# Two experts' tokens by halves of the sequence, in blocks that share one set of weights

## Chip, cores and metric

One core of one Trainium2 chip runs the whole program. The metric is the device time of one launch in microseconds; the kernel before took 1599.58 us (median of three runs, 1597.01 to 1599.73).

## What is computed

A decoder block on 1024 tokens of width 1024. A token mixer with two recurrent branches is followed by a mixture of experts and a final normalisation. Only the second part matters here:

```
g_logits = xf @ rg_w + rg_b;  grp = argmax(g_logits)            # 4 groups
e_logits = (xf @ re_w + re_b).reshape(T, 4, 8)
top_p, top_i = top_k(softmax(e_logits[t, grp]), 2)               # 2 experts of the group's 8
y[t] = sum over the 2:  weight * (silu(xb @ w_gate[e]) * (xb @ w_up[e])) @ w_down[e]
out = rmsnorm(h + y)
```

All is float32. There are 32 experts; the three matrices of one expert are 6 MB, and all of them, some 201 MB, are read from HBM in every launch.

## The kernel before

After the two branches, a loop `for hv in range(2)` (L971) takes the tokens in two halves of 512. For each half it does the up-projections (L997 to L999), then the output projection in four column quarters (`for q in range(4)`, L1012; matmuls L1025 to L1027). In the last quarter `begin` and `finish` (L934, L945) work off one chunk of 128 tokens at a time: transposes, norm, router logits `plg` (L950 and L957, float32 matmuls 128x36), and the normalised rows to `hf_dr` in HBM.

**Routing** runs in three groups of chunks, `GROUPS = ((0, 4), (4, 7), (7, 8))`. `choose` finds the two experts of each token, `place` counts ranks within an expert with two matmuls (L884, L885) and makes one-hot rows `oht` of each token's position; `spread` (L841) multiplies them with token numbers into a table `ptb`, one column of row numbers per expert. `pick` (L1070) then ranks the experts by their counts, writes the ranked expert numbers to `pei`, and `ranked` (L1092) permutes the table; `weigh` (L1108) does the same for the mixing weights.

**Blocks.** Three experts (29 to 31) are fixed: their weights are fetched before the counts are known, and each takes a block of up to 112 tokens. Of the other 29 the 11 with most tokens take full blocks (one of them a second one), and the other 18 share nine *paired* blocks, two experts with up to 64 tokens each. A full block splits each weight tile in a high and a low float32r part (`split`, L60 on ScalarE, L61 on VectorE) and does three matmuls of 512 columns; a paired block (`pair_mm`, L1356) multiplies the raw float32 tiles, with 64 stationary columns for each of the two experts. So a full block reads 6 weight tiles, a paired block 12.

**Weight tiles.** A tile is 128x2048 float32, 1,048,576 bytes (1.0486 MB); there are 192. `fetch` (L1240) puts them in order into a ring of 11 buffers (`rawxl`, `rawtg`, `rawoh`, `rawbo`, `rawxh`), whose memory earlier stages have used. All are issued in order from SyncE's queue: L1406 for experts known beforehand, L1413 for ranked ones, whose number SyncE first reads from `pei` into a register (L1410). A buffer comes free when its tile has been split, or when the pair's matmuls have read it.

**Order.** The program loops over 23 steps: three fixed blocks, then a pair followed by one or two full blocks, and a pair at the end. In step n it emits the gate and up matmuls (`pgu`), the next block's gather of rows from `hf_dr` by POOL (`gather`, L1263) and their transposes (`pxg`), and then the down matmuls (`pyd`) of step n-1 and the scatter-add of its result. A tile scheduler moves instructions within each engine's queue; each queue is then worked off in order. `overflow` (L1132, at n == 3) builds tables for blocks that did not fit; its loop at the end is entered only if there are any.

Of the kernel before, what the change touches and what calls it, by code (L numbers as in the profile page):

```python
# [9 lines left out]
F32 = mybir.dt.float32  # L10
# [22 lines left out]
def block_kernel(ctx, tc, x, meta_tokens, hg_lb_logits, norm_mix_g, w_in, gd_conv_w, gd_A_log, gd_dt_bias,  # L33
# [193 lines left out]
    ND = NE - 3  # L227
    NF = 11
# [590 lines left out]

    def first_max(name, vals, n, hot):  # L820
# [14 lines left out]
    def spread(oh, dst, n, ps=None, groups=GROUPS):  # L835

        ps = pr("ptb") if ps is None else ps
        for g in groups:
            for a in range(2):
                for c in range(*g):  # L840
                    nc.tensor.matmul(ps[:, 0:n], oh[a][:, c], dst[:, a * NC + c],  # L841
                                     start=(a == 0 and c == 0), stop=(a == 1 and c == NC - 1))
        return ps[:, 0:n]

    def choose(c0, c1):
# [5 lines left out]
        V.tensor_scalar(goh, goh, 1.0e30, -1.0e30, op0=ALU.mult, op1=ALU.add)  # L851
# [24 lines left out]
    def place(c0, c1):  # L876
# [22 lines left out]

    H = SEQ // 2  # L900
    ges = []
# [43 lines left out]
    def finish(cc, h2, hT, hf, ss):  # L945
# [3 lines left out]
        for k in range(6):  # L949
            nc.tensor.matmul(pl[:, 0:36], hT[:, k], wrt[:, k], start=(k == 0), stop=False)  # L950
# [5 lines left out]
        for k in range(6, 8):  # L956
            nc.tensor.matmul(pl[:, 0:36], hT[:, k], wrt[:, k], start=False, stop=(k == 7))  # L957
# [13 lines left out]
    for hv in range(2):  # L971
# [11 lines left out]
        for n in range(8):  # L983
# [7 lines left out]
            for j in range(2):  # L991
# [3 lines left out]
                for k in range(4):  # L995
# [9 lines left out]
                                   op0=ALU.mult, op1=ALU.subtract)  # L1005
        h2s = []
# [4 lines left out]
        for q in range(4):  # L1011
# [6 lines left out]
            qs = slice(q * 256, (q + 1) * 256)  # L1018
            for c in range(4):
# [16 lines left out]
        if hv == 0:  # L1036
            routed(*GROUPS[0])
    place(*GROUPS[1])
    ptb = pr("ptb")
    oht = ohts  # L1040
    spread(oht, ohb1, NE, ptb, GROUPS[:2])
    routed(*GROUPS[2])
    spread(oht, ohb1, NE, ptb, GROUPS[2:])


    tabi = r_("tabi", [P, NB], I32)
    wsl = r_("wsl", [P, NB])
    emp = r_("emp", [P, NB])

    def rows(ps, s):  # L1050
        V.tensor_scalar(emp[:, s], ps, 0.0, None, op0=ALU.is_equal)
        return V.scalar_tensor_tensor(tabi[:, s], emp[:, s], BIG, ps, op0=ALU.mult, op1=ALU.add)
# [3 lines left out]
    tabbed = rows(ptb[:, ND:NE], slice(NW, NBB))  # L1056
    tab1 = r_("tab1", [P, NE])
    V.tensor_copy(tab1, ptb[:, 0:NE])
    pei = r_("pei", [1, NE], I32)
    pef = r_("pef", [1, NE])  # L1060
    rowb = r_("rowb", [CL, NPR], I32)
# [8 lines left out]
    def pick(after):  # L1070

        with tc.issue_after(after.ins):
# [14 lines left out]
            t = ranked(tab1)  # L1087
            rows(t[:, 0:NW], slice(0, NW))
            V.tensor_scalar(ktmp[0:CL, 0:NPR], t[0:CL, NW:], 0.0, None, op0=ALU.is_equal)
            return V.scalar_tensor_tensor(rowb, ktmp[0:CL, 0:NPR], BIG, t[0:CL, NW:], op0=ALU.mult, op1=ALU.add)  # L1090

    def ranked(t):  # L1092
# [5 lines left out]
        o = ps[:, 256:256 + NW + NPR]  # L1098
# [4 lines left out]
        nc.tensor.matmul(o[0:CL, NW:], tT[:, 0:CL], perm[:, NF + NPR:ND], start=True, stop=True, skip_group_check=True)  # L1103
# [4 lines left out]
    def weigh(after):  # L1108

        with tc.issue_after(after.ins):  # L1110
# [12 lines left out]
            pw = spread(oht, ohw.rearrange("p a b e -> p a (b e)"), 2 * NE)  # L1123
            V.tensor_copy(tab1, pw[:, 0:NE])
            V.tensor_tensor(tab1, tab1, pw[:, NE:], op=ALU.add)
            V.tensor_copy(wsl[:, NW:NBB], tab1[:, ND:NE])
            V.tensor_copy(wsl[:, 0:NW], ranked(tab1)[:, 0:NW])
# [4 lines left out]
    def overflow():  # L1132

# [15 lines left out]
        V.tensor_tensor(pos, pos, psx, op=ALU.add)  # L1149
        gtx = r_("gtx", [P, NE, NT])  # L1150
# [72 lines left out]
    sx = mix.tile([P, 4, 1024], F32R, name="sx", tag="xh1")  # L1223
    whs = [sx[:, i] for i in range(2)] + [wp.tile([P, 1024], F32R, name=f"mwh{i}", tag="wh") for i in range(2)]
    wls = [sx[:, i + 2] for i in range(2)] + [wp.tile([P, 1024], F32R, name=f"mwl{i}", tag="wl") for i in range(2)]
    wls.append(tl.tile([P, 1024], F32R, name="mwl4", tag="gffn"))
# [11 lines left out]
    ring = list(range(len(raws)))  # L1238
# [10 lines left out]
    def raw(load, src, q):  # L1249
        nuse[0] += 1  # L1250
        return early.pop(0) if early else fetch(load, src, q)

    def wload(load, src, q):
        wr = raw(load, src, q)
        r = []
        for g in range(2):
            wh, wl = whs[next_("h", len(whs))], wls[next_("l", len(wls))]
            with tc.issue_after(tabbed.ins) if nuse[0] <= 6 else ExitStack():
                split(wh, wl, wr[g])
# [327 lines left out]
```

## Time and profile before

| what | value |
|---|---|
| runs | 1599.58, 1599.73, 1597.01 us |
| the profiled execution | 1599.57 us, span 1597.8 us |
| mean granted TensorE clock | 0.974 |
| busy: TensorE, VectorE, ScalarE, POOL | 94%, 50%, 34%, 12% |
| moved by DMA | 360.88 MB, of it 307.51 MB read from HBM |

The profile's times are counted from the span's start. Busy TensorE time is modelled: rows of matmuls overlap, so the distance between starts, not a row's duration, tells how fast they follow each other. A DMA share of 1.0 means that all 16 DMA engines worked all the time.

### The profile page before, as it was taken

The numbers are of one execution on the slowest core, as the hardware profiler recorded it, in microseconds if no ns is written. First come the engines' busy times: TensorE is split into PE (matmuls) and PEld (weight loads), VectorE is DVE, ScalarE is ACT, GpSimd is POOL, SyncE is SP. The second block draws the span as 40 slices with busy tenths as digits, with TensorE's granted clock in tenths as the row PEclk, the third lists the DMA queues.
The fourth block names the chain that finished last, engine by engine and source line by source line (L and its number), as shares of the span: only waits on it lengthen the run. The fifth ranks groups of instructions, "written<-read, shape, count | busy, mean of one in ns | idle before, by whom it ended". The sixth has DMA issues, their size and how long they took to land. (4 is left out here: it accounts for less than half of the span.)

```text
span 1597.8 us, 25202 instructions
## 1 busy us (share of the span) xinstructions
PE 1497.6 (94%) x9915; PEld 1136.9 (71%) x9915; DVE 803.1 (50%) x1512; ACT 540.8 (34%) x884; POOL 191.1 (12%) x161
## 2 busy tenths in 40 slices
PE   6999999999999999999999997898998988999984
PEld 6989898789888777778889797665545543655542
DVE  7223665458547638132455745865444431533635
ACT  6122321331232232223234323552444431533533
POOL 2050000010000001000000102115111111111013
PEclk9999999999999999999999997898999999999996
DMA  6264344335135324327765655798999999999995
GB/s 214 68 178 149 94 138 136 100 116 167 61 115 146 104 87 116 108 84 250 254 180 182 204 176 211 253 354 340 390 393 390 402 390 384 377 373 398 405 342 205
DMA packets 193387, 360.88 MB, mean 226 GB/s; under 512 B 29416, under 2 KB 136106, under 8 KB 168689
## 3 DMA queue, kind: packets, MB, share of 16 engines
q1 hardware_dynamic: 171872, 319.61, 56.1%
q0 software_dynamic: 6416, 16.42, 4.3%
q10 hardware_dynamic: 14976, 23.21, 4.2%
q8 instruction: 79, 1.29, 0.3%
q14 instruction: 44, 0.35, 0.1%
HBM read 307.51 MB, written 57.94 MB: 229 GB/s over the span
## 5 line engine op out<-in xcount | busy, mean ns | idle before, releaser
L287 PE MATMUL pj<-xh,wh 128*128 128x512 f32 (+2 forms) x832 | 307.5, 370 | 0.0
L289 PE MATMUL pj<-xh,wl 128*128 128x512 f32 (+2 forms) x832 | 306.9, 369 | 0.0
L288 PE MATMUL pj<-xl,wh 128*128 128x512 f32 (+2 forms) x832 | 305.7, 367 | 0.0
L287 PEld LDWEIGHTS pj<-xh,wh 128*128 128x128 f32 x832 | 156.7, 188 | 17.0 <-issue 0.2
L289 PEld LDWEIGHTS pj<-xh,wl 128*128 128x128 f32 x832 | 156.8, 188 | 16.6 <-issue 0.6
L288 PEld LDWEIGHTS pj<-xl,wh 128*128 128x128 f32 x832 | 156.6, 188 | 15.9
L347 ACT ACTIVATE st<-pj 128x512 f32<-128x512 f32 (+2 forms) x104 | 54.8, 527 | 169.7 <-PE pj L289 160.2
L61 DVE TENSOR_TENSOR wl<-wr,wh 128x1024 fp32r<-128x1024 f32 x44 | 53.7, 1221 | 85.4 <-ACT wh L60 75.4
L311 POOL TENSOR_TENSOR rn<-ss,mhalf 128x4 f32<-128x4 f32 x16 | 20.9, 1304 | 536.5 <-DVE ss L322 304.9
L60 ACT ACTIVATE wh<-wr 128x1024 fp32r<-128x1024 f32 x44 | 46.6, 1059 | 109.8 <-PE pj L288 97.6
L1025 PE MATMUL pyo<-wo,mm 128*128 128x256 f32 x256 | 73.5, 288 | 4.9 <-ACT mm L1003 4.9
L1026 PE MATMUL pyo<-wo,mm 128*128 128x256 f32 x256 | 72.8, 285 | 0.0
L1027 PE MATMUL pyo<-wo,mm 128*128 128x256 f32 x256 | 72.5, 285 | 0.0
L1358 PE MATMUL pgu<-rawxl,xTp 128*64 128x512 f32 x208 | 65.3, 604 | 4.8 <-DMA rawxl<-in_w_up_dram 4.8
L1371 DVE TENSOR_TENSOR msg<-msg,pgu 128x512 f32<-128x512 f32 x9 | 6.2, 688 | 119.8 <-PE pgu L1358 111.7
L1294 PE MATMUL pgu<-mwl,xTs 128*112 128x512 f32 x144 | 57.6, 401 | 2.3 <-DVE mwl L61 2.2
L1400 POOL DMA_INDIRECT h_dr<-h,tabi x23 | 37.8, 1643 | 167.8 <-ACT h L1336 86.6
L1025 PEld LDWEIGHTS pyo<-wo,mm 128*128 128x128 f32 x256 | 49.0, 192 | 5.3 <-ACT mm L1003 5.3
L997 PE MATMUL pup<-oh,uwh 128*128 128x512 f32 x128 | 51.8, 405 | 0.3 <-ACT uwh L60 0.3
L998 PE MATMUL pup<-ol,uwh 128*128 128x512 f32 x128 | 51.7, 404 | 0.0
L999 PE MATMUL pup<-oh,uwl 128*128 128x512 f32 x128 | 51.3, 402 | 0.3 <-DVE uwl L61 0.3
L1292 PE MATMUL pgu<-sx,xTs 128*112 128x512 f32 x120 | 49.6, 413 | 1.9 <-ACT sx L60 1.7
(651 smaller groups left out, 3272.9 us busy)
## 6 DMA issues: line engine op xcount, KB each, us to landing
rawxl<-in_w_up_dram SPq DMA_DIRECT2D x26, 1024.0 KB, 20.4
rawxl<-in_w_down_dram SPq DMA_DIRECT2D x23, 1024.0 KB, 21.1
wr<-in_w_in_dram SPq DMA_DIRECT2D x44, 512.0 KB, 4.5
rawxl<-in_w_gate_dram SPq DMA_DIRECT2D x22, 1024.0 KB, 24.8
rawxh<-in_w_down_dram SPq DMA_DIRECT2D x14, 1024.0 KB, 19.7
rawoh<-in_w_gate_dram SPq DMA_DIRECT2D x13, 1024.0 KB, 11.2
rawoh<-in_w_up_dram SPq DMA_DIRECT2D x12, 1024.0 KB
rawbo<-in_w_down_dram SPq DMA_DIRECT2D x12, 1024.0 KB, 22.3
```

The lines of the kernel that those rows point to most:

```text
L61: return eng.tensor_tensor(out=lo, in0=src, in1=hi.bitcast(F32), op=ALU.subtract)
L287: nc.tensor.matmul(ps[:, :n], wh[:, k], a, start=(k == 0), stop=False)
L288: nc.tensor.matmul(ps[:, :n], wh[:, k], b, start=False, stop=False)
L289: last = nc.tensor.matmul(ps[:, :n], wl[:, k], a, start=False, stop=(k == KD - 1))
L347: act(out=st[:, :n], in_=ps, func=func, scale=scale)
L997: nc.tensor.matmul(ps, wh[:, kk], oh[:, kk], start=(k == 0), stop=False)
L998: nc.tensor.matmul(ps, wh[:, kk], ol[:, kk], start=False, stop=False)
L1025: nc.tensor.matmul(ps[:, 0:256], mm[0][:, k, ts], wo[:, 0, k], start=(k == 0), stop=False)
L1026: nc.tensor.matmul(ps[:, 0:256], mm[0][:, k, ts], wo[:, 1, k], start=False, stop=False)
L1027: nc.tensor.matmul(ps[:, 0:256], mm[1][:, k, ts], wo[:, 0, k], start=False, stop=(k == 7))
L1294: nc.tensor.matmul(ps[:CB], xTh[:, kk], wl[:, s], start=False, stop=(kk == 7))
L1358: nc.tensor.matmul(ps[hs], lhsT[:, hs], w[2][:, s], start=start, stop=stop, skip_group_check=True)
```

## The change

The fixed experts are two now, 30 and 31 (`ND = 30`), and 12 experts instead of 11 take full blocks (`NF = 12`); nine pairs stay. Experts 30 and 31 together take two paired blocks: one for the tokens of the first half of the sequence, one for those of the second, each with up to 64 tokens of either expert, and the second uses the 12 weight tiles that were fetched for the first (`kept`). The table of the first half's block is spread at the end of hv == 0, its rows are gathered in hv == 1 into the buffer `rawtg` (tile `b1`), and are transposed ahead of the last quarter. The ring starts with 12 buffers (`rawxh` has four), and after 12 fetches goes on with `rawtg` and ten of them. The router's logits are computed in two halves of 64 tokens. The tables of `overflow` are split off and stand two steps later, behind that step's matmuls. The addition into `xg` (L1540) moves into the loop for overflow. Cut to its core:

```diff
-    ND = NE - 3
-    NF = 11
+    ND = NE - 2
+    NF = 12
...
-    def spread(oh, dst, n, ps=None, groups=GROUPS):
+    def spread(oh, dst, n, ps=None, groups=GROUPS, first=True, last=True):
...
+    def second(a, b):
+        return V.tensor_copy(tabB[CL:P, a - NF:b - NF], tabi[CL:P, a:b])
+    def fixed_rows(t, c):
+        for hs, e in zip(HALVES, (ND + 1, ND)):
+            V.tensor_copy(tabf[hs], t[hs, e:e + 1])
+        return rows(tabf, slice(c, c + 1))
...
         for k in range(6):
-            nc.tensor.matmul(pl[:, 0:36], hT[:, k], wrt[:, k], start=(k == 0), stop=False)
+            for hs in HALVES:
+                nc.tensor.matmul(pl[hs, 0:36], hT[:, k, hs], wrt[:, k], start=(k == 0), stop=False, skip_group_check=True)
...
+        if hv:
+            b1 = rawp.tile([P, 2, D], F32, name="b1", tag="tg")
+            nc.gpsimd.memset(b1[:, 0], 0.0)
+            gather(b1[:, 0], tabi[:, NW:NW + 1], P, H)
...
+            if hv and q == 3:
+                b1T = pair_x(b1[:, 0], b1[:, 1].rearrange("p (k t) -> p k t", k=KD))
...
         if hv == 0:
             routed(*GROUPS[0])
+            oht = ohts
+            V.tensor_copy(n0, off[:, 4, ND:])
+            V.tensor_copy(off[:, 4, ND:], off[:, 0, ND:])
+            ptb = spread(oht, ohb1, NE, groups=GROUPS[:1])
+            V.tensor_copy(tab1, ptb)
+            fixed_rows(tab1, NW)
+            second(NW, NW + 1)
     place(*GROUPS[1])
...
-    tabbed = rows(ptb[:, ND:NE], slice(NW, NBB))
+    tabbed = fixed_rows(ptb, NW + 1)
+    V.tensor_tensor(tab1, tab1, ptb[:, 0:NE], op=ALU.add)
...
-            pw = spread(oht, ohw.rearrange("p a b e -> p a (b e)"), 2 * NE)
+            for i, g in enumerate((GROUPS[:1], GROUPS[1:])):
+                pw = spread(oht, ohw.rearrange("p a b e -> p a (b e)"), 2 * NE, groups=g)
...
-    for pool, tag, n, b in ((mix, "xl", 4, 1), (rawp, "tg", 1, 1), (rawp, "oh", 2, 1), (tl, "bo", 2, 2), (mix, "xh0", 2, 1)):
+    for pool, tag, n, b in ((mix, "xl", 4, 1), (rawp, "oh", 2, 1), (tl, "bo", 2, 2), (mix, "xh0", 2, 1), (mix, "xh1", 2, 1),
+                            (rawp, "tg", 1, 1)):
...
+        if nraw[0] == NR:
+            ring[:] = [NR] + ring[:NR - 2]
...
-    steps = [(c,) for c in range(NBB - 1, NW - 1, -1)]
+    steps = [(NW,), (NW + 1,)]
...
         if c >= NW:
-            return by_expert(c - NW + ND)
+            loads = [by_expert(NE - 1), by_expert(ND)]
+            def both(src, q):
+                k = (src.tensor.name, q)
+                if k not in kept:
+                    kept[k] = [fetch(load, src, q) for load in loads]
+                return kept[k]
+            return both
...
-    xT = gathered(0)
-    first = xT[0][2]
+    xT = b1T
...
         if n == 0:
-            picked = pick(first)
+            picked = pick(tabbed)
+            weigh(picked)
...
         if n == 0:
-            weigh(picked)
+            down(*pend)
+            pend = None
         if n == 3:
             with tc.issue_after(picked.ins):
-                overflow()
+                over = overflow()
+        if n == 5:
+            with tc.issue_after(done_gu[0].ins):
+                overflow_tables(*over)
```

TensorE's queue at the end of the routing, before: the rank matmuls `prk`, the spreads into `ptb`, and then the first block (`pxg` are its transposes, `pgu` its gate matmuls).

```order
L884 MATMUL prk<-moh,ones 128x96
L885 MATMUL prk<-moh,tri 128x96
L841 MATMUL ptb<-ohb_7750,oht_8757 128x32 x4
L841 MATMUL ptb<-ohb_7750,oht_8758 128x32 x4
L841 MATMUL ptb<-ohb_7750,oht_8757 128x32 x3
L841 MATMUL ptb<-ohb_7750,oht_8758 128x32 x3
L884 MATMUL prk<-moh,ones 128x32
L885 MATMUL prk<-moh,tri 128x32
L841 MATMUL ptb<-ohb_7750,oht_8757 128x32
L841 MATMUL ptb<-ohb_7750,oht_8758 128x32
L1275 MATMUL pxg<-ident,h_9880 128x112 x8
```

The same place of the change (L886 and L887 are the rank matmuls, L843 the spread, L1408 the pair's matmuls, with `b_9197` the first half's transposed rows):

```order
L1408 MATMUL pgu<-rawxl,b_9197 64x512 x3
L1003 MATMUL plg<-wrt,hT 64x36 x4
L1408 MATMUL pgu<-rawxl,b_9197 64x512 x8
L886 MATMUL prk<-moh,ones 128x96
L887 MATMUL prk<-moh,tri 128x96
L1408 MATMUL pgu<-rawxl,b_9197 64x512 x5
L1408 MATMUL pgu<-rawoh,b_9197 64x512
L843 MATMUL ptb<-ohb_7752,oht_8799 128x32 x3
L843 MATMUL ptb<-ohb_7752,oht_8800 128x32 x2
L1408 MATMUL pgu<-rawoh,b_9197 64x512 x2
```

The gate and up matmuls of step 0 stand between the routing's matmuls. Behind these rows come one spread matmul, the second pair of `prk`, four `pgu`, the last two spread matmuls, and nine `pgu`; group 0's eight spread matmuls are gone from here.

TensorE's queue of the change somewhat later, from the last matmul of the weights' spread to the second block's up matmuls (`h_9978` are its gathered rows, `xTp_9991` their transposes; `phh` and `msg_9995` belong to step 0's hidden rows):

```order
L843 MATMUL ptb<-ohw,oht_8800 128x64
L1141 MATMUL prt<-ident,tab_7761 32x128
L936 MATMUL pxg<-ident,h_9978 128x128 x4
L1145 MATMUL prt<-perm,tT 128x12
L1147 MATMUL prt<-perm,tT 64x9 x2
L936 MATMUL pxg<-ident,h_9978 128x128 x4
L1429 MATMUL phh<-ident,msg_9994 128x128 x4
L1408 MATMUL pgu<-rawxl,xTp_9991 64x512
L1408 MATMUL pyd<-rawxh_9987,msg_9995 64x512 x8
L1408 MATMUL pyd<-rawxh_9988,msg_9995 64x512 x8
L1408 MATMUL pgu<-rawxl,xTp_9991 64x512 x15
```

The second block's transposes stand behind the permuted weights, and 16 down matmuls of step 0 stand in front of all but one of the second block's gate matmuls.

SyncE's queue of the change where the ranked experts begin:

```order
L1457 DMA rawxh_9988<-in_w_down_dram 128x2048 x2
L1461 TENSOR_LOAD pei
L1461 ISA x2
L1461 TENSOR_LOAD pei
L1461 ISA x2
L1464 ISA
L1464 DMA rawtg<-in_w_gate_dram 128x2048
L1461 TENSOR_LOAD pei
```

After two register loads and one fetch, the 28 other loads of expert numbers follow in one run, and the next fetch (into `rawxl`) stands behind them; before, the first ranked fetch stood behind six loads, and the others were scattered among later fetches.

## Rows read from the trace of the kernel before

**Rows 1.** The page's 40 slices, busy share of the DMA engines in tenths.

```profile
DMA  6264344335135324327765655798999999999995
```

**Rows 2.** Busy time by stretches: length, engines, granted clock, DMA share, GB/s.

```profile
980.00:1000.00 20.00, 8.56 (x48) 7.90 (x47) 15.23 (x70) 5.48 (x9) 8.75 (x7) 0.56 0.45 159
1000.00:1020.00 20.00, 16.07 (x67) 11.90 (x67) 14.19 (x23) 10.08 (x12) 2.98 (x3) 0.75 0.72 247
1020.00:1040.00 20.00, 19.81 (x112) 15.58 (x111) 18.37 (x45) 12.92 (x16) 2.02 (x2) 1.00 0.79 287
1060.00:1080.00 20.00, 20.00 (x98) 9.42 (x97) 9.10 (x10) 9.18 (x13) 2.55 (x2) 1.00 0.90 347
1100.00:1120.00 20.00, 19.69 (x80) 9.14 (x82) 4.40 (x11) 1.83 (x3) 7.34 (x9) 0.78 0.77 270
1120.00:1500.00 380.00, 356.06 (x1538) 196.65 (x1535) 163.96 (x168) 154.26 (x195) 54.32 (x38) 0.99 1.01 390
1350.00:1400.00 50.00, 47.31 (x213) 30.93 (x212) 26.62 (x27) 24.71 (x30) 4.24 (x3) 1.00 0.96 382
```

**Rows 3.** The same view, one stretch of 5 us.

```profile
1000.00:1005.00 5.00, 1.07 (x6) 1.10 (x7) 2.54 (x3) 0.05 (x1) 1.99 (x2) 0.50 0.75 249
```

**Rows 4.** Timeline of TensorE, routing: start, duration, instruction, [idle before, releaser].

```profile
981.99 1.71 PE L957 MATMUL plg<-wrt,hT 128*128 128x36 f32 x8
990.96 0.45 PE L884 MATMUL prk<-moh,ones 128*128 128x96 f32 x1 [7.26 <-DVE moh L860]
...
996.90 0.61 PE L841 MATMUL ptb<-ohb,oht 128*128 128x32 f32 x2 [1.22 <-DVE oht L898]
1003.93 1.73 PE L1275 MATMUL pxg<-ident,h 112*128 112x112 f32 x8 [6.42 <-DMA h<-hf_dr,tabi]
...
1018.94 0.21 PE L1081 MATMUL prk<-perm,pid 32*1 32x32 f32 x2
```

**Rows 5.** Timeline of TensorE, a pair's matmuls and the weights' spread.

```profile
1028.49 1.87 PE L841 MATMUL ptb<-ohw,oht 128*128 128x64 f32 x16
...
1064.12 3.60 PE L1358 MATMUL pgu<-rawbo,xTp 128*64 128x512 f32 x16
1067.56 3.60 PE L1358 MATMUL pgu<-rawxh,xTp 128*64 128x512 f32 x16
```

**Rows 6.** Timeline of VectorE, tables and picking.

```profile
997.74 0.16 DVE L1052 SCALAR_TENSOR_TENSOR tabi<-emp,ptb 128x3 int32<-128x3 f32 x1
...
1006.81 0.16 DVE L1073 TENSOR_SCALAR key<-keys 128x3 f32<-128x3 f32 x1
...
1008.04 0.23 DVE L1079 TENSOR_SCALAR perm<-io,rankc 32x32 f32<-32x32 f32 x1
...
1031.73 1.22 DVE L61 TENSOR_TENSOR sx<-rawbo,sx 128x1024 fp32r<-128x1024 f32 x1
...
1034.47 0.18 DVE L1127 COPY wsl<-prt 128x20 f32<-128x20 f32 x1
```

**Rows 7.** SyncE's register loads, line L1410, ns min/median/max, first and last start.

```profile
L1410 SPq TENSOR_LOAD <-pei x6: 267/272/477, 1020.6 to 1023.8; - x6
```

**Rows 8.** Timelines of POOL and TensorE, overflow tables.

```profile
1087.21 15.64 POOL L1185 TENSOR_SCALAR oht<-io,slot 128x128 fp32r<-128x128 f32 x16 [2.65 <-DVE xst L1166]
...
1096.76 0.61 PE L841 MATMUL ptb<-ohc,oht 128*128 128x72 f32 x4 [2.72 <-DVE ohc L1190]
```

**Rows 9.** Timeline of TensorE, logits 128 wide, and a short run 64 wide.

```profile
973.43 1.42 PE L950 MATMUL plg<-wrt,hT 128*128 128x36 f32 x12
974.68 1.07 PE L929 MATMUL phT<-ident,h 128*128 128x128 f32 x8
...
1034.04 0.28 PE L1101 MATMUL prt<-perm,tT 32*64 32x9 f32 x4
1034.18 0.26 PE L1103 MATMUL prt<-perm,tT 32*64 32x9 f32 x2
1034.36 0.49 PE L1293 MATMUL pgu<-mwh,xTs 128*112 128x512 f32 x1
```

More of the change, by code (lines that the diff above doesn't have):

```diff
@@ L833, in block_kernel @@
     ohef = ohe.rearrange("p a c e -> p (a c) e")
-    def spread(oh, dst, n, ps=None, groups=GROUPS):
+    def spread(oh, dst, n, ps=None, groups=GROUPS, first=True, last=True):
         ps = pr("ptb") if ps is None else ps
[L838 to L842, printed above, removed]
+        ac = [(a, c) for g in groups for a in range(2) for c in range(*g)]
+        for i, (a, c) in enumerate(ac):
+            nc.tensor.matmul(ps[:, 0:n], oh[a][:, c], dst[:, a * NC + c], start=first and i == 0,
+                             stop=last and i == len(ac) - 1)
         return ps[:, 0:n]
@@ L887, in place @@
             V.memset(off[:, 0], 0.0)
+            V.memset(off[:, 0, ND:ND + 1], float(CL))
         for c in range(HC):
@@ L956, in finish @@
         for k in range(6, 8):
-            nc.tensor.matmul(pl[:, 0:36], hT[:, k], wrt[:, k], start=False, stop=(k == 7))
+            for hs in HALVES:
+                nc.tensor.matmul(pl[hs, 0:36], hT[:, k, hs], wrt[:, k], start=False, stop=(k == 7), skip_group_check=True)
         V.scalar_tensor_tensor(lg[:, cc], pl[:, 0:36], rs, brt, op0=ALU.mult, op1=ALU.add)
@@ L1086, in pick @@
             V.tensor_scalar(nohx, ohx, -1.0, 1.0, op0=ALU.mult, op1=ALU.add)
[L1087 to L1090, printed above, removed]
+            rows(ranked(tab1), slice(0, NW))
+            return second(NF, NBB)
     def ranked(t):
@@ L1149, in overflow @@
         V.tensor_tensor(pos, pos, psx, op=ALU.add)
+        for a in range(2):
+            t8 = rp.tile([P, 4, 2], F32, name="t8", tag="t4")
+            V.tensor_tensor(t8, ohe[:, a, 4:, ND:], bc(n0[:, None, :], [P, 4, 2]), op=ALU.mult)
+            V.tensor_reduce(out=psx[:, a, 4:], in_=t8, op=ALU.add, axis=AX.X)
+        V.scalar_tensor_tensor(psx[:, :, 4:], pos[:, :, 4:], float(CB), psx[:, :, 4:], op0=ALU.is_ge, op1=ALU.mult)
+        V.tensor_tensor(pos[:, :, 4:], pos[:, :, 4:], psx[:, :, 4:], op=ALU.add)
         gtx = r_("gtx", [P, NE, NT])
@@ L1247, in fetch @@
         return wr
-    def raw(load, src, q):
-        nuse[0] += 1
-        return early.pop(0) if early else fetch(load, src, q)
     def wload(load, src, q):
-        wr = raw(load, src, q)
+        wr = fetch(load, src, q)
+        if not whs:
+            split_tiles()
         r = []
@@ L1338, in stage2 @@
         return pys
[L1341 to L1354 removed]
     def pair_mm(ps, lhsT, ws, s, start, stop):
         for hs, w in zip(HALVES, ws):
[L1358 removed]
+            mm = nc.tensor.matmul(ps[hs], lhsT[:, hs], w[2][:, s], start=start, stop=stop, skip_group_check=True)
+        return mm
     def pair_gu(xT, loads):
@@ L1384, in pair_down @@
         for q in range(2):
-            ws = [raw(load, wd_e, q) for load in loads]
+            ws = loads(wd_e, q)
             for k in range(2):
@@ L1450, in gathered, with places @@
         if paired(n):
-            return pair_x(*[got[i] for i in range(len(gq)) if gq[i][0] == n])
+            (xg,) = [got[i] for i in range(len(gq)) if gq[i][0] == n]
+            return pair_x(xg, xTp[next_("p", 2)])
         return [stage_x(got[i]) for i in range(len(gq)) if gq[i][0] == n]
-    for e, srcs in ((0, (wg_e, wu_e)), (1, (wg_e, wu_e)), (0, (wd_e,)), (2, (wg_e, wu_e))):
-        early += [(weights(e), src, q) for src in srcs for q in range(2)]
-    early = [fetch(*a) for a in early[:len(raws)]]
+    def places(c, n):
+        return [(tabi[:, c:c + 1], CL), (tabB[:, c - NF:c - NF + 1], P)] if paired(n) else [(tabi[:, c:c + 1], CB)]
     def down(n, *a):
@@ L1491, in block_kernel @@
     nc.sync.dma_start(out=gfin, in_=rowbc(final_norm_g[None, :], D))
-    idle = [i for i in range(len(raws)) if i not in ring] + ring
+    idle = [i for i in range(NR + 1) if i not in ring and i not in (NR - 2, NR - 1)] + ring
     accs = [raws[i] for i in idle[:NC]]
-    lridxs, lwcol = pend[1][0]
+    lplaces, lwcol = pend[1][0]
     LN = P if paired(len(steps) - 1) else CB
```

142 lines of the change are left out of this document (77 added, 65 removed).

## The prediction

> **What bounds the kernel now.** I read the page's 40 slices first, then the table of busy time by stretches, and only then timelines of the stretch in which the first expert blocks start. In the slices the reader sees the DMA share at nine tenths or more from about two thirds of the span on [rows 1]. The stretches say how full that is: from 1120 to 1500 us the engines are at 1.01 of their time and move 390 GB/s [rows 2]. So the expert blocks wait for weights: a tile of 1.0486 MB takes 1.0486 MB / 390 GB/s = 2.69 us there, while a full block's TensorE work is spread over six tiles and a pair's over twelve. TensorE's high busy share is no objection, since its rows overlap: eight pair matmuls follow each other in 3.44 us (1067.56 - 1064.12) though each row lasts longer [rows 5]. A pair's gate and up part is four such groups, 13.8 us of TensorE for eight tiles, which are 21.5 us of DMA.
>
> What can be saved therefore is time in which the DMA engines stand idle before the end. Before, that is 11.0 us of 980 to 1000, 5.6 of 1000 to 1020, 4.2 of 1020 to 1040, 2.0 of 1060 to 1080 and 4.6 of 1100 to 1120 [rows 2]. In the first of these the 11 buffers are full and no tile can be replaced; TensorE stands still for 7.26 us while VectorE chooses experts and for 6.42 us until the first gather lands [rows 4]. A tile's bytes are the same before and after, 192 tiles, so the change pays if the refill of the ring begins earlier, in proportion to what is loaded by then.
>
> **The change, part by part.** Times are in the clock of the trace before; the sum is against its profiled execution, 1599.57 us, which is also the median of the runs to 0.01.
>
> *Ahead of 984.* TensorE works without a gap here (no idle time stands in the first [rows 9]), so additions count in full. Eight spread matmuls of the first half move here from the routing: 16 of them took 1.87 us at most [rows 5], so 0.9 us. Eight transposes of the first half's block: 0.9 us (0.11 each, from the spacing of such rows in [rows 9], 974.68 on). The logits, in halves: 12 rows took 1.25 us 128 wide (974.68 - 973.43), 0.104 each; 64 wide, four rows take 0.14 us, 0.035 each, but the change of width costs about 0.11 (0.18 us until the next wide matmul, less two rows) [rows 9]. Per chunk there were 16 rows and are 32, with four changes of width: 32 x 0.035 + 4 x 0.11 - 16 x 0.104 = -0.1 us, for eight chunks -0.8. Bounds: without the cost of changes -4.4; if a 64-wide row took as long as a wide one, 8 x 16 x 0.104 = +13.3. I take the low price per row because that is the one row of this width with few columns. Sum of this part: **+1.0**. The memset and the gather of this block run on POOL at the start of the output projection and are covered by its first three quarters; the bytes are those of the first gather before.
>
> *Step 0 in the routing's gaps.* Eleven pair matmuls stand ahead of the first rank matmul: 11 x 0.43 = 4.7 us, inside the gap of 7.26. The six ahead of the spread wait beside VectorE's one-hot rows. Two and four more stand ahead of the last rank and spread matmuls and hold them by some 0.7 us: the last spread ends at 998.2, not 997.5 [rows 4]. Nine more take until 998.2 + 3.9 = 1002.1. The second block's rows can land as before, 6.2 us after their table (997.74 to 1003.93) [rows 4, 6], some 1005.2. So step 0's 13.8 us of gate and up work are hidden. But TensorE's queue is in order, and the tables for all ranked blocks and their weights now stand ahead of the second block's transposes. Before, from the matmul for `pei` to the last permuted weight, this took 1018.94 to 1034.47 = 15.5 us [rows 4, 6], with seven splits of 1.22 us in VectorE's queue between, 8.5 us in all [rows 6]. Those splits are gone from here. Bounds 7.0 and 15.5; I take 8.3, near the lower end, since the queue now holds nothing else but one more set of sums. 1002.1 + 8.3 = 1010.4. Transposes and their copies took 1.6 us before the first matmul at the low clock (x8 in [rows 4]); with the hidden rows' transposes and copy I take 2.7: 1013.1. Then 16 down matmuls of step 0, 6.9 us, stand ahead of the second block's gate matmuls: 1020.0. The first two buffers are free after eight of those: 1023.1. TensorE idles between these tables, and the granted clock, 0.56 in the stretch with such gaps [rows 2], stands partly at the 1.2 GHz level: +1.4. **The first buffer is refilled at 1024.5.** It cannot be before 1021.5: SyncE's queue has 30 register loads behind the picking at some 1003.3, 0.6 us each (five spacings in 3.2 us) [rows 7], and the refill stands behind them. With 15.5 in place of 8.3 it is 1031.7.
>
> *What follows.* From issue to bytes some 1.5 us (1.25 of the first 5 us after 1000 were empty [rows 3]): 1026.0. By 1040 the kernel before had landed 11 tiles and 247 and 287 GB/s over 20 us each, 10.7 MB, less some 1.9 MB of four gathers of 112 or 128 rows of 4 KB: 8.4 tiles, 19.4 in all [rows 2]. The change has 13 by 1026 (12, and the one in `rawtg`) and the same four gathers. 6.4 tiles more remain, x 2.69 = 17.2 us. Start of the saturated stretch 1040.0 - 1026.0 = 14.0 earlier. The 2.0 and 4.6 us of idle DMA after 1040 go: the second stands where TensorE waits for `oht` of the overflow tables, 16 instructions on POOL, and VectorE's `ohc` [rows 8], and those matmuls now stand two steps later behind finished inputs. A new stall comes: the two buffers that held the first down tiles (`rawxh`) are free only after the second block's down matmuls, and these stand behind the third block's gate and up part. From the first refill: 10.3 us for the rest of the gate and up part, 13.8 for the third block's, 2 for transposes, 3.4 for eight down matmuls, 1.5 to the bytes = 31.0; the DMA has work for 1.5 + 8 x 2.69 + 2.7 (about 1 MB of gathers and scatters) = 25.7. It stands still for **5.3 us** (bounds 0, if other transfers fill it, and 8). Together -14.0 + 17.2 - 6.6 + 5.3 = **+1.9**. Moving the last addition out of the way costs and saves nothing that counts: it ran beside the last writes to HBM. Scatters: one more, on POOL, which is mostly idle [rows 2].
>
> Sum: 1599.57 + 1.0 + 1.9 = 1602.5; taken as **1602**, no change that counts. About 0.2%, 3.2 us, is what a measurement of this kernel can tell from no change.
>
> **Rivals.** *The gains come without the stall.* The tables take their lower bound, so that the register loads decide (1021.5: -3.0), other transfers fill the 5.3 us, and the idle 3 us of 1350 to 1400 [rows 2], where the doubled full block ran next to another, do not come back because it now stands alone between pairs: 1602 - 3 - 5 - 3 = 1591. For it: step 0 fills TensorE's gaps. Against: two of the three are waits that the new queue orders make.
>
> *TensorE is the bound.* Then the 13.8 + 6.9 us of step 0 brought into the gaps would show in full: 1599.6 - 20.7 + 1.0 = 1580. Against it speak 1.01 of DMA over 380 us. The granted clock is 0.56 in the gap before and 1.00 from 1020 on, the 1.2 and 2.4 GHz levels mixed and the latter alone [rows 2]. The Trainium skill (TensorE: Matmul & The Clock Gate, "What's actually happening") says that the throttled clock is the default and that activity lifts it; by that rule matmuls in the gap help the clock too, which would count under this rival alone.
>
> *Narrow matmuls lengthen the stretch ahead of 984.* This is the slower side: if 64-wide rows cost 0.074 rather than 0.035, halfway to the wide ones, eight chunks cost 8 x (32 x 0.074 + 0.44 - 1.66) = 9 us, and the time is 1602 + 10 = 1612. It decides from 0.05 us a row on, where the part is +3. For it: rows double in number. Against: [rows 9]. The Trainium skill (TensorEngine Tiling, "Key Properties") says that a change of tiling mode drains TensorE. In the trace it costs some 0.11 us; priced at that with no gain on the rows, 32 changes would be 3.5 us.
>
> *The change does not do what it says* in so far as the early block is hidden but its weights are not released: that is the forecast itself.
>
> **How the numbers follow.** Forecast 0.48, of which 0.36 within 0.2% and 0.12 above, its own range 1597 to 1608; without the stall 0.22; TensorE 0.07; narrow matmuls 0.23. Faster: 0.22 + 0.07 = 0.29; same 0.36; slower 0.12 + 0.23 = 0.35. The range leaves out the TensorE case and the far ends: 1589 to 1613.
>
> **What would show it.** Right: `pgu` rows between the `prk` rows and no longer gap there; a first refill of `rawxl` at 1022 to 1027; a DMA share under 0.5 between 1000 and that time, and a dip of some 5 us around 1050; no dip at 1100. Wrong: last logits of the second half more than 3 us off 984, a refill ahead of 1021, or stretches after 1120 with a DMA share well under 1.

## The result, and the profile after

The changed kernel takes 1613.72 us (median, 1609.63 to 1614.34), the kernel before in the same comparison 1598.30 us (1596.75 to 1599.73). The ratio is 1.0091, interval 1.0071 to 1.0112: slower by 0.9%, which is 14.5 us by the ratio and 15.4 by the medians. That is 0.7 us above the upper end of the range given, and 12 us above the likeliest case; slower had a chance of 0.35. The profiled execution has a span of 1612.5 us, 14.7 more than before.

The first page line again is the DMA share in 40 slices of 40.3 us, to be held against [rows 1].

```profile
DMA  6264344336136225237847646589999998999994
```

From 968 us on, three slices read 6, 5 and 8, where those from 959 us on read 5, 7 and 9 before. The stretches (columns as in [rows 2]: length; TensorE, its weight loads, VectorE, ScalarE, POOL; clock; DMA share; GB/s) say where the engines stand still.

```profile
980.00:1000.00 20.00, 17.98 (x94) 7.24 (x92) 14.57 (x78) 2.02 (x3) 7.87 (x7) 0.91 0.70 257
1000.00:1020.00 20.00, 14.57 (x61) 9.21 (x59) 7.46 (x42) 1.19 (x2) 2.38 (x3) 0.66 0.34 110
1020.00:1040.00 20.00, 20.00 (x97) 8.44 (x93) 1.44 (x2) 1.45 (x3) 3.07 (x2) 1.00 0.54 200
1040.00:1060.00 20.00, 19.55 (x93) 7.35 (x93) 2.63 (x4) 2.71 (x5) 2.09 (x2) 1.00 0.66 258
1060.00:1080.00 20.00, 19.59 (x89) 12.08 (x87) 11.26 (x11) 9.97 (x12) 4.72 (x3) 1.00 0.95 355
1100.00:1120.00 20.00, 15.88 (x60) 7.32 (x57) 5.41 (x5) 5.45 (x7) 5.02 (x7) 0.87 1.02 413
1120.00:1500.00 380.00, 353.11 (x1527) 199.29 (x1525) 165.93 (x175) 154.85 (x196) 54.97 (x40) 0.98 1.00 388
1300.00:1350.00 50.00, 44.12 (x176) 26.12 (x175) 16.75 (x16) 15.97 (x19) 2.57 (x2) 0.93 0.92 350
```

TensorE is busier from 980 to 1000 us (17.98 against 8.56 us, at a granted clock of 0.91 against 0.56), as the change intends. But the DMA engines idle 13.2 us from 1000 to 1020, 9.2 from 1020 to 1040 and 6.8 from 1040 to 1060; the dip of 1100 to 1120 is gone, and a new one stands before 1350. Added up over stretches of 10 us from 980 to 1560, idle DMA time is 45.5 us, before 32.5: 13.0 of the 14.7 us. By places the difference is +7.6 up to 1040 us, +6.0 from 1040 to 1080, -4.7 from 1100 to 1120, +3.3 from 1300 to 1400 and +0.7 from 1500 on.

SyncE's timeline shows the two waits behind the first two of these: when which buffer is refilled.

```profile
1004.86 0.36 SPq L1464 DMA_DIRECT2D rawtg<-in_w_gate_dram  x1
1028.50 3.77 SPq L1464 DMA_DIRECT2D rawxl<-in_w_gate_dram  x3
1039.37 0.33 SPq L1464 DMA_DIRECT2D rawbo<-in_w_gate_dram  x1
1061.02 0.33 SPq L1464 DMA_DIRECT2D rawxh<-in_w_gate_dram  x1
```

And its waits from 1000 to 1064 us (in all, times, longest) name who released it.

```profile
SPq L1464 <- PE pyd L1408: 21.1, 1, 21.1
SPq L1461 <- DVE pei L1130: 16.6, 1, 16.6
SPq L1464 <- PE pgu L1408: 13.7, 4, 6.8
```

The first refill comes at 1028.50, 6.8 us after SyncE was ready for it (1021.7, behind its register loads): step 1's gate matmuls released it. The tile after `rawbo` waits 21.1 us for a `pyd` row, step 1's down part, and is issued at 1061.02. TensorE's timeline (columns as in [rows 4]) shows what stands ahead of both.

```profile
998.10 4.02 PE L1408 MATMUL pgu<-rawbo,b 128*64 128x512 f32 x15
1002.05 0.21 PE L1129 MATMUL prk<-perm,pid 32*1 32x32 f32 x2
...
1007.45 3.59 PE L843 MATMUL ptb<-ohw,oht 128*128 128x64 f32 x16 [3.49 <-DVE dsh L1188]
1012.10 0.40 PE L1141 MATMUL prt<-ident,tab 128*32 128x128 f32 x1 [1.05 <-DVE tab L1175]
1012.29 1.06 PE L936 MATMUL pxg<-ident,h 128*128 128x128 f32 x4
...
1017.70 7.77 PE L1408 MATMUL pyd<-rawxh,msg 128*64 128x512 f32 x30
...
1031.74 3.98 PE L1408 MATMUL pgu<-rawoh,xTp 128*64 128x512 f32 x16
...
1057.34 7.09 PE L1408 MATMUL pyd<-rawxh,msg 128*64 128x512 f32 x32
```

Step 0's gate matmuls fill the gaps to 1002.05 us. Then come the tables, with gaps of 3.49 and 1.05 us that VectorE ends, step 0's down part until 1025.3 us, step 1's gate and up part, step 2's from 1040.7 us, and only at 1057.34 step 1's down part.

What answers to [rows 9] is a chunk's logits, now 64 wide in 32 rows, between the output projection's rows, and the last logit row of all.

```profile
967.40 0.28 PE L1079 MATMUL pyo<-wo,mm 128*128 128x256 f32 x1
967.61 0.90 PE L995 MATMUL plg<-wrt,hT 128*64 128x36 f32 x24
968.43 0.98 PE L973 MATMUL phT<-ident,h 128*128 128x128 f32 x7
969.35 0.43 PE L1003 MATMUL plg<-wrt,hT 128*64 128x36 f32 x8
969.71 0.33 PE L973 MATMUL phT<-ident,h 128*128 128x128 f32 x1
969.80 0.37 PE L1077 MATMUL pyo<-wo,mm 128*128 128x256 f32 x1
...
982.86 0.23 PE L1003 MATMUL plg<-wrt,hT 128*64 128x36 f32 x1
```

The same chunk in the kernel before, from the last `pyo` row ahead of it to the first one behind it:

```profile
967.76 0.29 PE L1027 MATMUL pyo<-wo,mm 128*128 128x256 f32 x1
967.88 1.43 PE L950 MATMUL plg<-wrt,hT 128*128 128x36 f32 x12
969.14 1.07 PE L929 MATMUL phT<-ident,h 128*128 128x128 f32 x8
970.05 0.62 PE L957 MATMUL plg<-wrt,hT 128*128 128x36 f32 x4
970.50 0.37 PE L1025 MATMUL pyo<-wo,mm 128*128 128x256 f32 x1
```

It took 2.74 us (970.50 - 967.76) and takes 2.40 (969.80 - 967.40): 0.34 less, with twice the rows.

### The profile page after: what moved, and what is told of

The parts are those of the page before. It is cut to its first block, busy times and chain, and to the rows that moved or that the text cites. A ratio compares the mean times of both kernels' runs of the same rounds, so it can differ in the third digit from the quotient of the medians.

```text
span 1612.5 us, 25521 instructions
## 1 busy us (share of the span) xinstructions
PE 1510.1 (94%) x10087; PEld 1120.3 (69%) x10087; DVE 776.9 (48%) x1515; ACT 513.6 (32%) x856; POOL 190.2 (12%) x164
## 4 chain that ended last, share of the span: by engine, by line
PE 73%; DMA 13%; DVE 6%; issue 3%; ACT 3%; POOL 1%; SPq 0%; DVEq 0%; POOLq 0%; ACTq 0%
PE pj L287 9%; PE pj L289 9%; PE pj L288 9%; PE pgu L1408 5%; PE pyd L1408 4%; DMA rawxl<-in_w_down_dram 3%; DMA rawxl<-in_w_up_dram 3%; PE pgu L1358 3%; PE pgu L1356 2%; PE pgu L1357 2%; PE pyo L1077 2%; PE pyo L1078 2%; PE pyo L1079 2%; PE pup L1045 1%; DMA rawbo<-in_w_down_dram 1%
## 5 line engine op out<-in xcount | busy, mean ns | idle before, releaser
L289 PEld LDWEIGHTS pj<-xh,wl 128*128 128x128 f32 x832 | 156.8, 189 | 16.7 <-issue 0.6
L1408 PE MATMUL pgu<-rawxl,xTp 128*64 128x512 f32 x224 | 71.4, 640 | 10.8 <-DMA rawxl<-in_w_up_dram 10.8
L1408 PEld LDWEIGHTS pgu<-rawxl,xTp 128*64 128x64 f32 x224 | 21.6, 146 | 51.5 <-issue 36.3
L1358 PE MATMUL pgu<-mwl,xTs 128*112 128x512 f32 x130 | 52.3, 404 | 3.6 <-DVE mwl L61 3.4
```

The source lines that it names most:

```text
L289: last = nc.tensor.matmul(ps[:, :n], wl[:, k], a, start=False, stop=(k == KD - 1))
L1358: done_gu[0] = nc.tensor.matmul(ps[:CB], xTh[:, kk], wl[:, s], start=False, stop=(kk == 7))
L1408: mm = nc.tensor.matmul(ps[hs], lhsT[:, hs], w[2][:, s], start=start, stop=stop, skip_group_check=True)
```

## The experiments

The theory going in: what is lost is DMA time, in two waits of the ring of buffers, for its first refill and for `rawxh`. The rivals: narrow matmuls, or an order elsewhere. Two things bear on every reading. The stretch ahead of the routing ends earlier or later from one profile to the next (the last logit row starts between 979.5 and 985.4 us in eleven profiles with the same code there), so positions count to some 3 us only, differences within one profile to less. And "idle DMA" is again the sum over stretches of 10 us.

| run | edit | median us | ratio to the kernel before, interval |
|---|---|---|---|
| u_logits_wide | logits 128 wide again | 1613.11 | 1.0092, 1.0075 to 1.0109 |
| a_down0_after_gu1 | step 0's down later | 1611.94 | 1.0083, 1.0064 to 1.0102 |
| r_ring | other order of buffers | 1607.30 | 1.0054, 1.0038 to 1.0071 |
| b_both | downs of steps 0 and 1 ahead of step 2 | 1601.79 | 1.0023, 1.0013 to 1.0033 |
| bw_weigh_later | b_both, weights' tables later | 1595.29 | 0.9988, 0.9977 to 0.9998 |
| bwr_loads_spread | and register loads spread | 1596.89 | 0.9992, 0.9979 to 1.0005 |
| arw_ring_order | tables later, down 0 later, buffers | 1590.75 | 0.9958, 0.9942 to 0.9973 |
| arwg_fulls_moved | and full blocks moved | 1589.92 | 0.9951, 0.9934 to 0.9967 |
| d_down_before_double | down ahead of the doubled block | 1613.78 | 1.0106, 1.0089 to 1.0123 |
| o_overflow_together | overflow tables back | 1613.97 | 1.0097, 1.0079 to 1.0115 |
| arwo_overflow_together | the same in arw_ring_order | 1591.19 | 0.9957, 0.9940 to 0.9975 |
| bt_tables_behind_down | kernel before, tables one step later | 1596.62 | 0.9993, 0.9980 to 1.0005 |

**Narrow logits undone** (u_logits_wide), in both places:

```diff
-            for hs in HALVES:
-                nc.tensor.matmul(pl[hs, 0:36], hT[:, k, hs], wrt[:, k], ...
+            nc.tensor.matmul(pl[:, 0:36], hT[:, k], wrt[:, k], start=(k == 0), stop=False)
```

> The changed kernel with the router's logits 128 wide again, in one matmul per k. By my theory (the loss is idle DMA time from 1000 to 1061 us, set by the refill and by the hold on rawxh) this costs what the narrow rows saved, some 0.8 us: 1613.7 + 0.8 = 1614.5, between 1612 and 1617, with the idle DMA stretches moved by that and no shorter. By the rival that narrow matmuls lengthen the stretch ahead of 984 us it gets faster by some 9 us: 1605.

1613.11 us: no difference to the change, and not 1605. In its profile a chunk like the one above takes 2.73 us again, in place of 2.40, and the stretch from the first `pyo` row of the second half to the last logit row is 63.3 us, against 59.2 after, 1.7 of it from a clock of 0.83 in one stretch of 10 us. Narrow rows save time there, they cost none. The rival falls.

**The two waits, one by one.** In a_down0_after_gu1 the down part of step 0 follows step 1's gate and up part:

```diff
-        if n == 0:
-            down(*pend)
-            pend = None
```

> The changed kernel, but step 0's down part is issued after step 1's gate and up part. By my theory the first rawxl refill comes at about 1021.7 us instead of 1028.5 (the register loads on SyncE then decide), but the time follows the release of rawxh, which still stands behind step 2's gate and up part: 1057.6 instead of 1061.0, so the time falls by about 3.4 us only, 1610, and the DMA dip near 1050 gets longer (10 us or so in place of 8). If the refill alone decides, the time falls by 6.8 us, 1607. If neither matters (rival: what bounds is elsewhere), 1613 to 1615.

1611.94 us. Its SyncE timeline:

```profile
1022.59 3.77 SPq L1464 DMA_DIRECT2D rawxl<-in_w_gate_dram  x3
1060.21 0.33 SPq L1464 DMA_DIRECT2D rawxh<-in_w_gate_dram  x1
```

By position the refill comes 5.9 us earlier and `rawxh` 0.8. But the last logit row starts at 985.4 us in this profile and at 982.9 in the changed kernel's; counted from it, the refill comes 8.5 us earlier (expected 6.8) and `rawxh` 3.4, as expected. The time falls by 1.8 us; whether that is less than the 3.4 expected, four runs that lie 5 us apart cannot tell. The idle time moves from the first wait to the second, 43.2 us in all against 45.5: the refill alone does not decide. In r_ring no matmul moves; the ring takes `rawxh` four tiles later:

```diff
         if nraw[0] == NR:
-            ring[:] = [NR] + ring[:NR - 2]
+            ring[:] = [NR] + ring[:NR - 4]
+        if nraw[0] == NR + 13:
+            ring[:0] = [NR - 4, NR - 3]
```

> The changed kernel with another order of buffers: the 22nd to 25th tiles go to rawtg and the first three of rawxl, and rawxh is taken four tiles later. No matmul moves. By my theory the first refill stays at 1028.5 us, the next tile after rawbo is issued at about 1044 us instead of 1061, the dip near 1050 us (8.2 us) goes, and the time falls by 6 to 8 us: 1605.5 to 1608. If the dip is paid for elsewhere, or other waits take its place, 1613.

1607.30 us, 6.4 less. Its SyncE timeline:

```profile
1028.71 3.77 SPq L1466 DMA_DIRECT2D rawxl<-in_w_gate_dram  x3
...
1044.57 0.33 SPq L1466 DMA_DIRECT2D rawtg<-in_w_gate_dram  x1
...
1060.99 0.91 SPq L1466 DMA_DIRECT2D rawxh<-in_w_down_dram  x2
```

`rawxh` is free no earlier than before, but nothing waits for it: the next tile goes out at 1044.57 to `rawtg`. The DMA share from 1040 to 1070 is full and idle DMA falls from 45.5 to 39.0 us, 6.5, much as the time does. So the hold on `rawxh` is shown by itself. With both waits shortened (b_both; its order of instructions puts step 1's down part ahead of step 2):

```diff
-        if n == 0:
+        if n == 1:
             down(*pend)
             pend = None
```

> The changed kernel, with the down parts of steps 0 and 1 both issued after step 1's gate and up part, ahead of step 2's. By my theory rawxh is released at about 1042.6 us, before the eight tiles ahead of it have landed (1047), the dip near 1050 us goes and the refill comes at about 1021.7: 6.8 + 8.2 = 15 us less, 1598 to 1600, level with the kernel before. If only the refill matters, 1607; if only the hold on rawxh, 1605.5; if neither, 1613 to 1615.

1601.79 us, 11.9 less, not 15: the refill comes at 1022.28, but `rawxh` at 1045.81 rather than 1042.6, and the late dip stays.

```profile
1022.28 3.77 SPq L1464 DMA_DIRECT2D rawxl<-in_w_gate_dram  x3
...
1045.81 0.33 SPq L1464 DMA_DIRECT2D rawxh<-in_w_gate_dram  x1
```

The reason written for 1021.7 was wrong here. SyncE waited 6.3 us for a `pgu` row before the refill, so it was ready at 1016.0: only 17 register loads stand ahead of it in this kernel, and TensorE set the refill.

**The weights' tables.** In bw_weigh_later they are computed in step 1:

```diff
-            weigh(picked)
...
+        if n == 1:
+            weigh(picked)
         if pend is not None:
             down(*pend)
```

> As b_both, and the tables of the blocks' weights (the L843 spread of ohw and its ranked copy) are also computed later, behind step 1's gate and up part. Step 1's gate and up part then starts some 6 us earlier (1009 in place of 1016 us). By my theory the first refill stays where it was, at 1022 us, because SyncE's 28 register loads end there, and only the later tiles come sooner: 1600 to 1602 us against 1601.8 of b_both. If TensorE's tables alone decided the refill, it would come at some 1012 to 1014 us and the time would be 1592 to 1594.

1595.29 us, 6.5 under b_both, where no difference was expected. Its SyncE timeline:

```profile
1007.59 3.77 SPq L1464 DMA_DIRECT2D rawxl<-in_w_gate_dram  x3
...
1036.43 0.33 SPq L1464 DMA_DIRECT2D rawxh<-in_w_gate_dram  x1
```

The refill comes 14.7 us earlier than in b_both (13.0 counted from the last logit row). Here one register load stands ahead of it: the loads go where the instruction order has room, and were no bound. The tables were: they kept TensorE from step 1 from 1002.05 to 1012.29 us, with the second block's rows landed (in bw_weigh_later its transposes start at 1001.64). To make sure of the loads, bwr_loads_spread pins each behind an earlier tile:

```diff
-        er = nc.values_load(ix, engines=[mybir.EngineType.SP], ...
+        with tc.issue_after(fetched[-4].ins) if main else ExitStack():
+            er = nc.values_load(ix, engines=[mybir.EngineType.SP], ...
```

> As bw_weigh_later, and SyncE loads the experts' numbers step by step, each behind the fourth last tile issued before, in place of 28 register loads in one run ahead of the first refill. By my theory the refill now comes when step 1's first matmuls are done, 1012 to 1014 us, 8 to 10 us ahead of b_both, and nothing holds the next tiles: 1592 to 1594 us, faster than the kernel before by 0.3%. If register loads are not what holds the refill, the time is that of bw_weigh_later. If the tiles that come earlier are only waited for later (a longer dip near 1040 to 1050 us), 1598 to 1601.

1596.89 us and a refill at 1009.60: the time of bw_weigh_later. The loads did not hold it.

**Both waits and the tables** (arw_ring_order): `weigh` as above, no `down` of step 0 ahead of step 1, and the ring with `NR + 15`.

> Weights of the blocks computed later as in bw_weigh_later, step 0's down part behind step 1's gate and up part as in a_down0_after_gu1 (step 1's stays behind step 2's), and the buffers in another order: tiles 22 to 27 go to rawtg, rawxl and rawoh, and rawxh is taken six tiles later than in the changed kernel. By my theory the first refill comes at 1008 to 1010 us as in bw_weigh_later, no tile waits for rawxh before it is needed, and the dip of 4.3 us at 1030 to 1040 us that bw_weigh_later still has goes: 1591 us, 0.4% under the kernel before. If TensorE's work piles up there instead (the buffers full, a dip between 1050 and 1110 us), 1594 to 1597.

1590.75 us, 0.42% under the kernel before (interval 0.27 to 0.58). The SyncE timeline and the stretch from 1030:

```profile
1008.03 3.77 SPq L1466 DMA_DIRECT2D rawxl<-in_w_gate_dram  x3
...
1034.31 0.33 SPq L1466 DMA_DIRECT2D rawtg<-in_w_gate_dram  x1
```

```profile
1030.00:1040.00 10.00, 10.00 (x48) 3.47 (x44) 0.75 (x1) 1.88 (x3) 1.48 (x1) 1.00 0.76 272
```

The dip there is 2.4 us, in bw_weigh_later 4.3: smaller, not gone. With its buffers free in time and the weights' tables later, the changed kernel is faster than the kernel before. That the early block makes this gain is not shown: no run computes the weights' tables later, or orders the ring anew, in the kernel before.

**The late dip.** In the changed kernel SyncE waits 12.9 us for a `pyd` row ahead of 1352 us, and 5.3 us are idle from 1340 to 1360.

```profile
SPq L1464 <- PE pyd L1408: 15.2, 2, 12.9
```

```profile
1340.00:1350.00 10.00, 10.00 (x50) 6.93 (x50) 1.98 (x3) 1.08 (x2) 1.05 (x1) 1.00 0.57 235
```

d_down_before_double issues the down part ahead of the doubled block:

```diff
-        if n == len(steps) - 1:
+        if pend is not None and (n == len(steps) - 1 or len(steps[n]) > 1):
             down(*pend)
```

> The changed kernel, with the down part of the step ahead of the doubled full block issued before that block's gate and up part. By my theory the dip of the DMA share at 1340 to 1360 us (5.3 us idle) is the same kind of hold: SyncE waits 12.9 us there for rawbo, read by that down part. It should shrink to under 1.5 us and the time fall by 3 to 4 us, to 1610. If the dip comes from TensorE being the bound there, it stays, or moves by a step, and the time stays at 1613 to 1614.

1613.78 us: no gain. Its waits of SyncE from 1310 to 1380 us, and a stretch:

```profile
SPq L1464 <- PE pgu L1408: 19.0, 8, 11.8
```

```profile
1350.00:1360.00 10.00, 10.00 (x51) 5.95 (x51) 3.15 (x5) 2.17 (x4) 1.07 (x1) 1.00 0.61 225
```

The wait for `pyd` is gone and one of 11.8 us for `pgu` has its place; the dip moved by 10 us (0.61, 3.9 us idle). My theory of a hold falls here. TensorE is busy throughout the dip, which speaks for TensorE as the bound around the doubled block, but that is argued. arwg_fulls_moved tried to relieve it:

```diff
-        a, b = (NF * c // (NPR - 1) for c in (c, c + 1))
+        a, b = ((0, 2, 3, 5, 6, 7, 8, 10, 12, 12)[c] for c in (c, c + 1))
```

> As arw_ring_order, and of the full blocks between the pairs 2, 1, 2, 1, 1 (the doubled one), 1, 2, 2 stand in place of 1, 2, 1, 2, 1 (the doubled one), 2, 1, 2, so that the doubled block has one full block less on either side. If the late dip (4.9 us at 1320 to 1340 us in bw_weigh_later) comes of TensorE's work piled up around the doubled block, it should shrink to 2 to 3 us, and the time lie 2 us under arw_ring_order. If it comes of the doubled block alone (its six tiles take twice the TensorE time), it stays and the times agree within 1 us.

1589.92 us, 0.8 under arw_ring_order, within the intervals; the dip from 1310 to 1330 us goes from 5.9 to 4.9 us. Differences of this size say little, since the late dip varies between profiles with the same order of steps: from 1300 to 1400 us 5.9 us are idle in arw_ring_order and 3.5 in arwo_overflow_together (below), 5.6 in the changed kernel and 3.1 in o_overflow_together. Inconclusive: what makes the late dip stays open.

**The overflow tables.** The prediction took 4.6 us off because their matmuls stand later. o_overflow_together puts them back:

```diff
-                over = overflow()
-        if n == 5:
-            with tc.issue_after(done_gu[0].ins):
-                overflow_tables(*over)
+                overflow_tables(*overflow())
```

> The changed kernel with the overflow tables' matmuls put back to where they were, in the same step as the overflow's VectorE and GpSimd work. By my theory TensorE waits again for some 5 to 8 us behind that work near 1100 us, the DMA dip of 4.6 us that the kernel before had comes back, and the time rises to 1617 to 1618. If the saturated DMA absorbs the wait, 1613 to 1614.

1613.97 us. TensorE's timeline and a stretch:

```profile
1098.32 1.04 PE L843 MATMUL ptb<-ohc,oht 128*128 128x72 f32 x4 [3.63 <-DVE ohc L1252]
1100.36 4.37 PE L843 MATMUL ptb<-ohc,oht 128*128 128x72 f32 x12 [1.00 <-POOL oht L1247]
```

```profile
1100.00:1110.00 10.00, 9.10 (x29) 5.28 (x31) 2.61 (x9) 0.54 (x1) 7.92 (x11) 0.50 1.01 419
```

TensorE waits 4.6 us, in the kernel before 4.5, and the DMA does not notice. Was that because the DMA was late? In arw_ring_order it is not, so the same edit was made there.

> As arw_ring_order, with the overflow tables' matmuls back in the step of the overflow's VectorE and GpSimd work, as in o_overflow_together. There the same wait of TensorE (3.63 + 1.00 us for ohc and oht) cost nothing. If that was because the DMA had restarted so late that TensorE was the one ahead, it should cost here, where TensorE hardly waits for tiles between 1060 and 1110 us: a DMA dip of 3 to 5 us behind the wait, and 1593 to 1595 us against 1590.75. If the buffers absorb the wait wherever it comes, the time stays within 1.5 us of arw_ring_order, and no dip shows.

1591.19 us against 1590.75, no dip (1.02, 1.02 and 0.98 from 1080 to 1110 us), with waits of TensorE of 4.0 us in all, the longest:

```profile
1092.28 4.37 PE L843 MATMUL ptb<-ohc,oht 128*128 128x72 f32 x12 [2.52 <-POOL oht L1247]
```

The buffers absorb it in either case. In the kernel before, SyncE's longest wait from 1080 to 1120 us is of another kind:

```profile
SPq L1413 <- PE pyd L1358: 18.6, 2, 17.2
```

It waited for a pair's down part that stood behind the tables. bt_tables_behind_down moves only the tables' matmuls, in the kernel before, behind that down part:

```diff
+        return ohc, xend, xb
+
+    def overflow_tables(ohc, xend, xb):
         po = spread(oht, ohc, 3 * NX)
...
+        if n == 4:
+            with tc.issue_after(done_gu[0].ins):
+                overflow_tables(*over)
```

> The kernel before, with one thing of the change: the overflow tables' 16 matmuls and what follows them stand one step later, behind the down part of the first pair, in place of ahead of it. In the kernel before SyncE waits 17.2 us for that down part (tiles in rawbo), which starts at 1105 us, behind the tables (1096.8 to 1103.3 us, with the waits for ohc and oht) and at the low clock; the DMA is idle for 4.7 us from 1100 to 1120. If the place of the tables ahead of that down part makes the dip, the down part comes some 8 us earlier, the dip goes, and the time falls by 4 to 5 us: 1593. If the dip comes of the step's length and not of the tables, it stays, and the time is 1597 to 1599.

The dip is gone and the longest wait for `pyd` 5.2 us:

```profile
1100.00:1110.00 10.00, 10.00 (x54) 4.34 (x55) 3.19 (x9) 0.98 (x2) 4.67 (x5) 1.00 1.02 364
1110.00:1120.00 10.00, 9.28 (x44) 4.41 (x41) 2.56 (x4) 2.87 (x4) 2.99 (x2) 1.00 1.02 350
```

So the place of the tables ahead of the down part made that dip. The time is 1596.62 us against 1598.04, a ratio whose interval holds 1: a gain of 4 to 5 us is not seen. Idle DMA falls by 3.2 us in the profile, not 4.7, since some of it returns later (0.6 us from 1370 to 1380, 0.6 from 1520 to 1540). Why the median shows less than that is open.

## Why the prediction was right and wrong

*The bound* was right. Edits that shortened a wait of the ring moved the time by about the idle DMA time they removed: r_ring 6.4 for 6.5 us, b_both 11.9 for 11.5, bw_weigh_later 18.4 for 18.7. In arw_ring_order it is 23.0 for 18.3 as the sum is taken, but its last fetch is issued at 1537.9 us (in the changed kernel at 1559.4); summed to 1540 us it is 23.0 for 22.2. The two that only gave TensorE a wait moved nothing (o_overflow_together, arwo_overflow_together).

*Ahead of 984* was right in sum as far as it can be read: the last logit row starts at 982.9 us, before at 983.3, and within each profile the second half's stretch, from its first `pyo` row to that row, is 59.2 us, before 58.0. Its term for the logits, -0.8, was too small: 0.34 us a chunk would make -2.7 for eight. The changes of width cost what they were priced at, 0.11 us each. The rows were mis-sized. 24 narrow rows last 0.90 us and a single one 0.23 (the last, at 982.86), so that they follow each other in 0.67 / 23 = 0.029 us and not in 0.035; a wide row takes 0.107 on average (16 in 1.71) and not 0.104. A chunk's 2.40 us less 0.12 to the first row, 0.91 for the transposes and 32 x 0.029 leave 0.44 for four changes. The Trainium skill (TensorEngine Tiling (Array Packing), "Key Properties") says that a change of tiling mode drains TensorE; the trace agrees that one costs something, 0.21 us from the last wide row's start to the first narrow one where 0.12 is usual.

*Step 0 in the gaps* was right: the tables start behind its last `pgu` at 1002.05 us, forecast 1002.1.

*The tables, 8.3 us, near the lower bound*, is the first step that failed. They took 12.2 us, from 1002.05 to the copy of the last permuted weight at 1014.24, just above the middle of the bounds. The queue held nothing else, as argued, but VectorE's own chain left gaps of 3.49 and 1.05 us, and the 16 spread matmuls took 3.59 us where [rows 5] had 1.87, at the low clock (0.57 from 1006 to 1008 us, 0.50 from 1008 to 1012). The transposes overlapped the end of them, and step 0's down part began at 1016.8, not 1013.1; it took 8.5 us, not 6.9, its first part again at the low clock, which is 0.50 to 0.51, the 1.2 GHz level, from 1010 to 1020 us and 1.00, the 2.4 GHz level, from then on. The eight matmuls after it took 3.2 us, where 3.1 and 1.4 for the clock stood. 3.7 + 1.6 - 1.3 = 4.0 us: 1028.5 in place of **1024.5**. The lower bound that the register loads would set (1021.5) was met, 1021.7, and did not count.

*The new stall of 5.3 us* was foreseen with its cause and its place, and is 8.2 us; `rawxh` came 32.5 us after the first refill, not 29.5, chiefly because step 2's gate and up part, from 1040.7 to the down part at 1057.3, took 16.7 us where 13.8 stood: eight transposes of the next block stand among it, and a wait of 0.45 us for a tile. Its upper bound of 8 was the better value.

*The stall of 4.6 us that goes* did go, 4.7, but the reason was incomplete: in the changed kernel the tables could have stayed (o_overflow_together). What cost was tables ahead of a down part that held buffers.

*The late dip* was put at nothing in the sum. It stood only in a rival, as a gain of 3 us that I expected if the doubled block stood alone (its row gives 2.0 us: a share of 0.96 over 50). It grew to 5.3 us instead, +3.3 over the stretch from 1300 to 1400; but o_overflow_together, with the same order of steps there and the same time, has +0.8, so this term is known to some 2.5 us only, and its cause is open.

So the sum's DMA part, +1.9, reads +13.0 when measured: 4.4 more for the refill and what lies before it, 2.7 for the stall, 3.3 for the late dip and 0.7 at the end. All err to the same side: the tables had been taken near their lower bound, the stall below what it measured, and the late dip at nothing. Of the rivals, narrow matmuls fell (u_logits_wide), and so did TensorE as the bound of the whole; the gains without the stall were reached, at 1590.75 us, but only with another order of buffers and matmuls.

## What to carry to other kernels

When blocks share weights to start early, ask of each buffer who reads it last, and where that reader stands in the queue: a tile that two steps share is free only after the second, and a ring that reaches it in order stands still although other buffers are free. Put such buffers last in the ring, and keep tables that no next matmul needs out of TensorE's queue ahead of the matmuls that free a buffer. Count an idle stretch of TensorE only if a buffer waits for it.

## What the runs showed of the hardware that was not expected

24 logit rows of 36 columns, 64 wide, take 0.82 us from the first to the matmul behind them, and 12 rows 128 wide take 1.26, so two narrow rows are cheaper than one wide one. The two halves of one k start 0.007 us apart, and such pairs follow each other every 0.058 us, wide rows every 0.112. With all changes of width a chunk takes 2.40 us in place of 2.74. The clock's price in short stretches is large: after TensorE's gaps of 3.49 and 1.05 us, a down part took 8.5 us in place of 6.9, and 16 small matmuls took 3.59 us in place of 1.87. The Trainium skill (TensorE: Matmul & The Clock Gate, "What's actually happening") says that the throttled clock is the default and that activity lifts it; the trace agrees: the clock is 0.50 behind the gaps, and 1.00 from 1020 us on, with matmuls following each other from 1012.3. And with the ring full of requests, waits of TensorE of 4.0 and 4.6 us left no mark on the DMA share.
